# Two partition sums moved behind column tiles, in a one-core hybrid decoder layer

## The chip, the core and the metric

The kernel runs on one core of a Trainium2 chip. The metric is the device time of one execution in microseconds. A core has five engines with a queue each: TensorE (PE in the profile; PEld is its loading of stationary weights), VectorE (DVE), ScalarE (ACT), GpSimd (POOL) and SyncE (SP, which issues DMAs here). TensorE writes its results to PSUM, eight banks of 128 partitions by 512 float32 numbers each; VectorE and ScalarE read them from there ("evacuate" them), GpSimd can't.

## What the kernel computes

One decoder layer on 512 tokens of width 2048, in float32:

```
xn = rms_norm(h, attn_norm_w);  proj = xn @ w_in
y  = [attention(c_q, c_kv, k_rope), conv_module(conv_in), hgrn2(hq, hf, hi, hg)]
h  = h + concat(y) @ w_out
xn = rms_norm(h, ffn_norm_w)
h  = h + (silu(xn @ w_gate) * (xn @ w_up)) @ w_down
return rms_norm(h, final_norm_w)
```

`rms_norm(x, w)` is `x * rsqrt(mean(x*x) + eps) * w`. The factor is one number per token, so it can be put on behind the matrix product: the kernel multiplies the raw `x * w` by the weights and scales each result by the factor, `rstd`, when it evacuates it. The convolution module splits its 1024 columns into `a` and `gate`, forms `a * sigmoid(gate)`, runs a causal convolution of width 31 over the tokens for each of 512 channels, a layer norm over the channels and `silu`. HGRN2 is a gated linear recurrence of four heads.

## The kernel before

Activations lie transposed, channels on the partitions and 512 tokens along the free dimension; a width of 2048 is 16 tiles (`KT`). Each float32 operand is split into a high part (`h`, rounded, by ScalarE, L136 or L139) and a low part (`l`, the rest, by VectorE, L137 or L140), and `mm3` (L143 to L147) forms a product from three matmuls: high by high, high by low, low by high.

`cols_tile` (L149) makes one column tile, 128 output channels by 512 tokens, in one bank of the tag `mm`: 16 k-tiles by 3 are 48 matmuls, with two weight loads of 512 KB. `weights` (L127) loads, splits and hands out these weights; it is traced at a priority 6000 steps ahead of its place, so that loads and splits run ahead as far as the buffers (two raw, three high, three low) allow. `rows_tiles` (L160) makes four banks at once, 192 matmuls.

The order within each engine's queue is fixed when the program is compiled. A planner walks through modelled time and gives each engine the instruction of highest priority that is ready; priority is the place in the program, moved by `high_priority`. The slots of one tag in a pool are handed out in the order of the program. A new area on the same side of memory takes over the place of the closed one, and a tile there waits until the older tiles in its place are done.

The first stage, `first` (L253), loads the 16 tiles of `x` and computes four column tiles of the convolution (`banks[0]` to `banks[3]`: gate and a of the blocks 0 and 1) in the four `mm` banks, k by k, 192 matmuls. Beside it ScalarE squares each `x` tile and GpSimd adds the squares to `acc` (L273). `x_norm` (L279) then sums `acc` over the partitions with a matmul by a matrix of ones (`sum_over_partitions`, L195, bank tag `ax` with two slots), runs `rsqrt` (L180, Ln and Exp on ScalarE, a Newton step on VectorE, then a copy on GpSimd) into `rstd`, and forms the same sums as a column for each token (L286, eight small matmuls, the other `ax` slot) into `rstd_r`. All of it is traced 2000 steps ahead of its place.

`conv_tile` (L435) evacuates a gate bank times `rstd` (L438), forms the sigmoid, evacuates the `a` bank (L443) and runs the 31 taps on VectorE (L449) at a priority 3000 steps behind its place. Blocks 2 and 3 get their banks from two `cols_tile` each. Then come the four banks of the values (tags `lv`, `lv`, `mm`, `mm`; `lv` has two slots), the four of the gate rows, the end of the convolution module with two more sums over the partitions (L452 to L471), and the four HGRN heads, whose tiles (area `hgrn`) take the place of the convolution's (area `conv`). Each head starts with two column tiles (`q`, L337, and `z`, L339).

Later, `project` (L663) makes the 16 column tiles of `w_out`, adds them to `h` and squares the result in the same manner (L680, L681). `project_end` (L684) sums the squares, forms the factor and copies it into `rstd` (L693); its scratch lies in the area `rest`. `token_sums` (L697 to L719), on VectorE and ScalarE, forms sums of quarters of `h` for a product scheme with fewer multiplications; its scratch (area `sum`) takes the place of `rest`. Two plain tiles of the feed-forward stage follow (`ff_plain`, a gate and an up tile each, four column tiles of 48), then 42 fast ones (`ff_fast`), whose first loads (L748) and whose outputs lie where `hf` was, the tile that `token_sums` reads. The lines that the change touches:

Of the kernel before, what the change touches and what calls it, by code (L numbers as in the profile page):

```python
# [92 lines left out]
class Trunk:  # L93
# [52 lines left out]
        mm(out, a[0], b[1], start=False, stop=False, **k)  # L146
        mm(out, a[1], b[0], start=False, stop=last, **k)  # L147

    def cols_tile(self, w, rhs):  # L149

        bank = self.ps("mm")
        n = len(rhs)
        for k0 in range(0, n, 8):
            h, l = self.weights(next(w))
            for k in range(k0, k0 + 8):
                s = slice((k - k0) * P, (k - k0 + 1) * P)
                self.mm3(bank, (h[:, s], l[:, s]), rhs[k], k == 0, k == n - 1)
        return bank
# [117 lines left out]
                self.mm3(banks[j], (h[:, s], l[:, s]), self.x[k], k == 0, k == KT - 1)  # L276
        return banks

    def x_norm(self, r1):  # L279
        nc = self.nc  # L280
        t = [r1(i) for i in ("rv", "ry", "rq")]
        total = self.sum_over_partitions(self.acc)
        nc.gpsimd.tensor_copy(self.rstd, self.rsqrt(total, D, "eps", *t))
        bank = self.ps("ax")
        for c in range(NB):
            nc.tensor.matmul(bank[:, c:c + 1], self.acc[:, c * P:(c + 1) * P], self.ones[:, :1],  # L286
                             start=True, stop=True)
        nc.vector.tensor_copy(self.rstd_r, self.rsqrt_small(bank[:, :NB], D))
# [438 lines left out]
        nc.vector.tensor_tensor(u, u, g, op=ALU.mult)  # L727
        nc.sync.dma_start(self.ffd[f], u)

    def ff_plain(self, f, w, fp):  # L730
        nc = self.nc
        gbank = self.cols_tile(w, self.hw)
        ubank = self.cols_tile(w, self.hw)
        g, u = fp("g"), fp("u")
        nc.vector.tensor_tensor(g, gbank, self.rstd, op=ALU.mult)
        self.last_silu = nc.scalar.activation(g, g, AF.Silu)
        nc.vector.tensor_tensor(u, ubank, g, op=ALU.mult)
        nc.sync.dma_start(self.ffd[f], u)
# [157 lines left out]
    def run(self):  # L896
        tc, io = self.tc, self.io
        area = lambda name, bufs, side="left", space=None: Area(tc, name, bufs, side, space)
        stream = lambda name: iter([io[name][i] for i in range(io[name].shape[0])])
        wr, wc, wa = stream("w_rows"), stream("w_cols"), stream("w_attn")  # L900
        self.mix, self.mix_y = [], []
        self.ps = area("banks1", {"mm": 4, "lv": 2, "ax": 2}, space=PSUM)
        self.yd = self.dp.tile([8, P, S], F32, name="yd")
        self.xp = area("xw", {"xh": KT, "xl": KT})
        self.keep = area("keep", {"h": 4, "l": 4, "krh": 1, "krl": 1, "sin": 1, "cos": 1}, "right")
        r1 = area("conv", {"xraw": 3, "xsq": 2, "acc": 1, "vt": 2, "vsig": 2, "cg": 1, "csg": 2, "hpad": 4,
                           "cacc": 4, "csum": 2, "csq": 2, "cmu": 1, "rv": 1, "ry": 1, "rq": 1,
                           "pos": 1, "ang": 1, "rn": 1, "rr": 1}, "right")
        self.consts()
        banks = self.first(r1, stream("w_first"))  # L910
        self.more_consts()
        self.rope_tables(r1)
        with tc.high_priority(offset=2000):
            self.x_norm(r1)
        self.lower_bounds()
        conv = [self.conv_tile(r1, banks[0], banks[1], 0), self.conv_tile(r1, banks[2], banks[3], 1)]
        for i in (2, 3):
            gbank = self.cols_tile(wc, self.x)
            abank = self.cols_tile(wc, self.x)
            conv.append(self.conv_tile(r1, gbank, abank, i))  # L920
        self.hgrn_values(wr, r1)
        self.hgrn_gates(wr, r1)
        self.conv_end(r1, conv)
        r1.close()
        r2 = area("hgrn", {"lmask": 1, "vh": 2, "gh": 1, "ps": 2, "qk": 2, "e": 2, "ls": 1, "st": 1, "E": 4,
                           "kr": 1, "state": 1, "og": 1, "lt": 5, "la": 1, "lb": 1, "lv_": 1}, "right")
        self.lmask = r2("lmask", I32, (P, len(LEVELS) * 64 + P))
        self.nc.gpsimd.dma_start(self.lmask, io["lmask"])
        for i in range(HG):
            self.hgrn_head(r2, wc, i)  # L930
        cq = self.latent(wc, r2, "lt")
        self.latent_norm(cq, r2)
        self.cq = self.latent_split(cq, "q_w", self.keep)
        ckv = self.latent(wc, r2, "lt")
        self.latent_norm(ckv, r2)
        self.k_rope(wc, r2)
        self.xp.close()
        self.mx = area("mix", {"mx": 2 * KT})
        ckvn = area("ckvn", {"h": 4, "l": 4})
        self.ckv = self.latent_split(ckv, "kv_w", ckvn)  # L940
        r2.close()
        self.ps.close()
        self.ps = area("banks2", {"sc": 2, "mm": 3, "tb": 2, "ob": 1}, space=PSUM)
        r3 = area("attn", {"cmask": 1, "v": 8, "knh": 2, "knl": 2, "qnh": 2, "qnl": 2, "qre": 2, "qro": 2,
                           "qraw": 1, "sw": 1, "rt": 1, "p": 3, "pt": 3, "og": 2, "o2": 1, "yr": 1}, "right")
        self.cmask = r3("cmask", F32, (P, P))
        self.nc.gpsimd.dma_start(self.cmask, io["cmask"])
        self.attention(wa, r3)
        r3.close()
        self.keep.close()  # L950
        ckvn.close()
        stat = area("stat", {"rms": 1, "epsv": 1}, "right")
        self.rms, self.epsv = stat("rms"), stat("epsv")
        self.hp = area("hw", {"hh": KT, "hl": KT}, "right")
        whole = area("whole", {"hf": 1}, "right")
        self.hf = whole("hf", F32, (P, KT, S))
        r4 = area("rest", {"acc": 1, "sq": 2}, "right")
        self.project(stream("w_out"), r4)
        self.ps.close()
        self.ps = area("banks3", {"mm": 8}, space=PSUM)  # L960
        self.project_end(r4)
        r4.close()
        self.mx.close()
        sp = area("sums", {"sh": 4, "sl": 4})
        tp = area("sum", {"s": 1}, "right")
        self.ffd = self.dp.tile([NF, P, S], F32, name="ffd")
        wg = stream("w_gu")
        self.token_sums(sp, tp)
        tp.close()
        whole.close()  # L970
        fp = area("gu", {"g": 2, "u": 2, "pa": 2, "pb": 2, "pc": 2}, "right")
        for f in range(PLAIN):
            self.ff_plain(f, wg, fp)
        rp = area("raw4", {"raw": 5, "t2": 1}, "right")
        for f in range(PLAIN, NF):
            self.ff_fast(f, wg, rp, fp)
        rp.close()
        fp.close()
        self.hp.close()
        sp.close()  # L980
        self.ps.close()
        self.ps = area("banks4", {"mm": 6, "ax": 2}, space=PSUM)
        late = area("late", {"h": 1}, "right")
        self.h = late("h", F32, (P, KT, S))
        fp = area("ff", {"fr": 3, "fh": 2 * CF, "fl": 2 * CF})
        lp = area("last", {"wlh": 10, "wll": 10, "mx": 8}, "right")
        r5 = area("ffn", {"v": 1, "y": 1, "sq": 3, "acc": 1}, "right")
        self.down_all(stream("w_down"), fp, r5, lp)
        for a in (r5, lp, fp, late, stat, self.ps):
            a.close()  # L990
# [115 lines left out]
```

## Time and profile before

| | |
|---|---|
| time, median of 3 executions | 2164.87 us (2163.61 to 2164.97) |
| profiled execution, its own time | 2165.62 us |
| its span in the profile | 2163.8 us, mean granted TensorE clock 0.988 of full |
| TensorE busy | 2111.9 us, 98% |
| VectorE, ScalarE, GpSimd busy | 1391.6 (64%), 893.8 (41%), 171.3 us (8%) |
| HBM read, written | 226.24, 24.12 MB, 116 GB/s over the span |

Times of instructions are counted from the start of the span. A row gives what an engine did, at which line of the kernel, on which tiles; in brackets stands how long the engine had been idle before it, and whose work ended that wait. `x2` behind a float32 sum means two instructions for one matmul of the code.

### The profile page before, as it was taken

The page shows a single profiled execution, that of the slowest core. Times are in us where ns is not written, and L with a number is a line of the kernel's source. Part 1 is how long each engine was busy: PE and PEld are TensorE (multiplying, and loading weights), DVE is VectorE, ACT ScalarE, POOL GpSimd, SP SyncE. Part 2 cuts the span into 40 slices and gives each one's busy share as a digit, 9 for nine tenths or more (in the row PEclk, how much of TensorE's full clock was granted, in tenths as well). Part 3 has the DMA queues.
Part 4 walks back from the last instruction along what each step waited for, and adds up shares of the span by engine and source line. Part 5 has one row for each costly group of instructions (what it writes and reads, how often), then busy time and mean ns, then how long its engine had stood idle before and what let it go on. Part 6 is the DMA issues. An engine that isn't in the chain of part 4 may idle for free.

```text
span 2163.8 us, 31928 instructions
## 1 busy us (share of the span) xinstructions
PE 2111.9 (98%) x13060; PEld 1894.6 (88%) x13060; DVE 1391.6 (64%) x1786; ACT 893.8 (41%) x1357; POOL 171.3 (8%) x150
## 2 busy tenths in 40 slices
PE   7999999999999999999999999999997999999997
PEld 6888888878878779999999999999997788888886
DVE  7897785556543377777787777778776443443347
ACT  6324763456453344444444444444443222221223
POOL 4102474100011100000000000000000000000001
PEclk9999999999999999999999999999999999999998
DMA  5233422222153334334433433433435442342332
GB/s 184 96 118 98 147 74 88 90 82 74 49 193 120 121 122 127 117 103 132 126 106 121 132 112 109 132 122 103 127 122 180 136 135 95 135 135 96 101 108 98
DMA packets 89907, 252.43 MB, mean 117 GB/s; under 512 B 9424, under 2 KB 17872, under 8 KB 89760
## 3 DMA queue, kind: packets, MB, share of 16 engines
q1 hardware_dynamic: 76528, 228.00, 33.0%
q10 hardware_dynamic: 13120, 22.03, 2.9%
q8 instruction: 102, 1.67, 0.3%
q0 software_dynamic: 112, 0.36, 0.1%
q14 instruction: 45, 0.37, 0.1%
HBM read 226.24 MB, written 24.12 MB: 116 GB/s over the span
## 4 chain that ended last, share of the span: by engine, by line
PE 92%; DVE 2%; DMA 2%; ACT 2%; POOL 1%; issue 1%; SPq 0%; DVEq 0%; ACTq 0%; POOLq 0%
PE mm L145 28%; PE mm L147 28%; PE mm L146 28%; PE lv L374 1%; PE ob L611 1%; PE lv L147 1%; PE lv L145 1%; PE lv L146 1%; DVE mx L862 1%; PE sc L586 1%; PE sc L587 1%; DMA xraw<-in_x 0%; DMA fr<-ffd 0%; PE tb L603 0%; ACT wh L136 0%
## 5 line engine op out<-in xcount | busy, mean ns | idle before, releaser
L136 ACT CAST wh<-raw 128x1024 fp32r<-128x1024 f32 (+1 forms) x463 | 478.3, 1035 | 834.5 <-PE mm L146 768.2
L137 DVE TENSOR_TENSOR wl<-raw,wh 128x1024 fp32r<-128x1024 f32 (+1 forms) x463 | 566.6, 1225 | 323.0 <-ACT wh L136 322.6
L146 PE MATMUL mm<-sl,wh 128*128 128x256 f32 x1344 | 378.3, 283 | 0.0
L145 PE MATMUL mm<-sh,wh 128*128 128x256 f32 x1344 | 378.1, 283 | 0.0
L147 PE MATMUL mm<-sh,wl 128*128 128x256 f32 x1344 | 373.5, 283 | 0.0
L145 PE MATMUL mm<-hh,wh 128*128 128x256 f32 (+1 forms) x1072 | 307.9, 287 | 0.0
L147 PE MATMUL mm<-hh,wl 128*128 128x256 f32 (+1 forms) x1072 | 307.5, 287 | 0.0
L146 PE MATMUL mm<-hl,wh 128*128 128x256 f32 (+1 forms) x1072 | 307.1, 286 | 0.0
L145 PE MATMUL mm<-fh,wh 128*128 128x512 f32 (+1 forms) x688 | 263.3, 386 | 12.9 <-ACT fh L136 9.7
L146 PE MATMUL mm<-fl,wh 128*128 128x512 f32 (+1 forms) x688 | 264.5, 385 | 0.2 <-DVE fl L137 0.2
L147 PE MATMUL mm<-fh,wl 128*128 128x512 f32 (+1 forms) x688 | 264.0, 384 | 0.0
L145 PEld LDWEIGHTS mm<-sh,wh 128*128 128x128 f32 x1344 | 257.3, 191 | 0.2 <-DVE u L790 0.2
L146 PEld LDWEIGHTS mm<-sl,wh 128*128 128x128 f32 x1344 | 257.5, 192 | 0.0
L147 PEld LDWEIGHTS mm<-sh,wl 128*128 128x128 f32 x1344 | 254.7, 192 | 0.0
L809 DVE TENSOR_TENSOR h<-h,mm 128x512 f32<-128x512 f32 x80 | 54.8, 687 | 238.2 <-PE mm L147 238.2
L146 PEld LDWEIGHTS mm<-hl,wh 128*128 128x128 f32 x1072 | 202.1, 189 | 3.3 <-issue 0.5
L147 PEld LDWEIGHTS mm<-hh,wl 128*128 128x128 f32 x1072 | 201.6, 188 | 2.9
L145 PEld LDWEIGHTS mm<-hh,wh 128*128 128x128 f32 x1072 | 201.7, 188 | 2.7 <-issue 0.2
L145 PE MATMUL mm<-xh,wh 128*128 128x512 f32 x400 | 160.6, 402 | 5.7 <-ACT wh L136 5.7
L145 PEld LDWEIGHTS mm<-fh,wh 128*128 128x128 f32 x688 | 130.6, 190 | 39.5 <-ACT fh L136 9.9
L146 PE MATMUL mm<-xl,wh 128*128 128x512 f32 x400 | 159.0, 397 | 1.3 <-DVE xl L140 1.3
L147 PE MATMUL mm<-xh,wl 128*128 128x512 f32 x400 | 156.9, 395 | 0.0
(330 smaller groups left out, 3242.6 us busy)
## 6 DMA issues: line engine op xcount, KB each, us to landing
raw<-in_w_gu SPq DMA_DIRECT2D x176, 512.0 KB, 4.3
raw<-in_w_down SPq DMA_DIRECT2D x88, 512.0 KB, 3.3
raw<-in_w_cols SPq DMA_DIRECT2D x42, 512.0 KB, 3.3
raw<-in_w_out SPq DMA_DIRECT2D x32, 512.0 KB, 3.3
ffd<-u SPq DMA_DIRECT2D x44, 256.0 KB, 3.9
fr<-ffd ACTq DMA_DIRECT2D x44, 256.0 KB, 3.6
raw<-in_w_rows SPq DMA_DIRECT2D x16, 512.0 KB, 3.3
raw<-in_w_attn SPq DMA_DIRECT2D x14, 512.0 KB, 3.4
```

Source lines behind the costliest of these rows:

```text
L136: nc.scalar.copy(h, src)
L137: nc.vector.tensor_tensor(l, src, h.bitcast(F32), op=ALU.subtract)
L145: mm(out, a[0], b[0], start=first, stop=False, **k)
L146: mm(out, a[0], b[1], start=False, stop=False, **k)
L147: mm(out, a[1], b[0], start=False, stop=last, **k)
L374: nc.tensor.matmul(bank[:, c * 64:(c + 1) * 64], e[:, c * P:(c + 1) * P], ap_of(e, c * P + h, [2 * h, 64 // h], [1, h]), start=True, stop= ...
L586: nc.tensor.matmul(bank[:, :n], q[rs, qs], k[1][rs, :n], start=False, stop=False)
L587: nc.tensor.matmul(bank[:, :n], q[:, qs], k[0][:, :n], start=False, stop=True)
L611: nc.tensor.matmul(obank[:, qs], pt[:, js], vt[h // 4, j][:, hs], start=j == 0, stop=j == i)
L809: nc.vector.tensor_tensor(self.h[:, m], self.h[:, m], bank, op=ALU.add)
L862: nc.vector.scalar_tensor_tensor(o[:, i * n:(i + 1) * n], self.h[:, m + i, ts], self.col("final_w", m + i), r, ALU.mult, ALU.mult)
```

## The change

Two sums over the partitions get a later place in the program. In the first stage, the two column tiles of convolution block 2 are traced ahead of the sum of `acc`, into the two `lv` banks instead of `mm`; the sum itself leaves `x_norm` and the priority that goes with it, while the rest of `x_norm` keeps both. Behind the projection, the first gate tile is traced ahead of `project_end` and handed to `ff_plain`.

```
-    def cols_tile(self, w, rhs):
-        bank = self.ps("mm")
+    def cols_tile(self, w, rhs, tag="mm"):
+        bank = self.ps(tag)
...
-    def x_norm(self, r1):
+    def x_norm(self, r1, total):
         t = [r1(i) for i in ("rv", "ry", "rq")]
-        total = self.sum_over_partitions(self.acc)
...
-    def ff_plain(self, f, w, fp):
-        gbank = self.cols_tile(w, self.hw)
+    def ff_plain(self, f, w, fp, gbank=None):
+        if gbank is None:
+            gbank = self.cols_tile(w, self.hw)
...
         self.rope_tables(r1)
+        early = [self.cols_tile(wc, self.x, "lv") for _ in range(2)]
+        total = self.sum_over_partitions(self.acc)
         with tc.high_priority(offset=2000):
-            self.x_norm(r1)
+            self.x_norm(r1, total)
...
         for i in (2, 3):
-            gbank = self.cols_tile(wc, self.x)
-            abank = self.cols_tile(wc, self.x)
+            gbank, abank = early if i == 2 else [self.cols_tile(wc, self.x) for _ in range(2)]
...
         self.ps = area("banks3", {"mm": 8}, space=PSUM)
+        wg = stream("w_gu")
+        gbank = self.cols_tile(wg, self.hw)
         self.project_end(r4)
...
-        wg = stream("w_gu")
         self.token_sums(sp, tp)
...
-            self.ff_plain(f, wg, fp)
+            self.ff_plain(f, wg, fp, gbank if f == 0 else None)
```

## Rows read from the trace of the kernel before

**Rows 1.** The page, part 1: busy time, share of the span, instructions.
```profile
PE 2111.9 (98%) x13060; PEld 1894.6 (88%) x13060; DVE 1391.6 (64%) x1786; ACT 893.8 (41%) x1357; POOL 171.3 (8%) x150
```

**Rows 2.** Waits of TensorE: line, waited for; us in total, times, longest.
```profile
PE ax L197 <- POOL acc L273: 4.5, 1, 4.5
PE mm L197 <- POOL acc L681: 4.0, 1, 4.0
...
PE ax L399 <- POOL E L393: 2.0, 1, 2.0
```

**Rows 3.** Timeline of TensorE, first place: start us, length us, engine, line, operation.
```profile
41.03 0.39 PE L147 MATMUL mm<-xh,wl 128*128 128x512 f32 x1
45.94 2.08 PE L197 MATMUL ax<-acc,ones 128*128 128x512 f32 x2 [4.53 <-POOL acc L273]
47.81 1.71 PE L286 MATMUL ax<-ones,acc 128*128 128x1 f32 x8
49.38 0.77 PE L145 MATMUL mm<-xh,wh 128*128 128x512 f32 x1
...
62.49 0.39 PE L145 MATMUL mm<-xh,wh 128*128 128x512 f32 x1
```

**Rows 4.** Groups of TensorE up to 41.5 us: count, busy us, mean ns, idle.
```profile
L145 PE MATMUL mm<-xh,wh 128*128 128x512 f32 x47 | 19.4, 413 | 5.7 <-ACT wh L136 5.7
```

**Rows 5.** Busy time by engine, first evacuation to last tap (window, length, engines, clock).
```profile
61.40:186.90 125.50, 125.50 (x555) 103.94 (x554) 120.75 (x159) 36.74 (x43) 11.60 (x6) 1.00 0.32 105
```

**Rows 6.** The same view: two stretches behind the sums; PEclk is third from last.
```profile
43.55:53.79 10.24, 7.85 (x20) 5.85 (x21) 7.82 (x12) 4.48 (x9) 2.26 (x2) 0.50 0.31 102
760.35:763.77 3.42, 3.42 (x9) 2.34 (x8) 1.92 (x3) 1.42 (x3) 0.00 (x0) 0.51 0.10 38
```

**Rows 7.** Timeline, second place: TensorE, ScalarE and VectorE.
```profile
755.48 0.39 PE L147 MATMUL mm<-mx,wl 128*128 128x512 f32 x1
755.68 1.04 ACT L136 CAST wh<-raw 128x1024 fp32r<-128x1024 f32 x1 [4.38 <-PE mm L146]
...
759.82 1.52 PE L197 MATMUL mm<-acc,ones 128*128 128x512 f32 x2 [3.95 <-POOL acc L681]
...
760.38 1.39 PE L145 MATMUL mm<-hh,wh 128*128 128x512 f32 x1
...
766.73 1.22 DVE L710 TENSOR_TENSOR s<-hf 128x1024 f32<-128x1024 f32 x1
```

**Rows 8.** Timeline of VectorE and GpSimd, first place.
```profile
44.09 2.35 DVE L137 TENSOR_TENSOR wl<-raw,wh 128x512 fp32r<-128x512 f32 x2
...
54.31 0.61 POOL L283 COPY rstd<-rv 128x512 f32<-128x512 f32 x1 [8.42 <-DVE r L188]
...
61.40 0.69 DVE L438 TENSOR_TENSOR cg<-mm,rstd 128x512 f32<-128x512 f32 x1 [1.39 <-PE mm L147]
```

**Rows 9.** The chain that ended last, at the convolution's first sum.
```profile
193.90 0.86 PE ax L197 x2
```

**Rows 10.** Timeline of GpSimd and VectorE: convolution's last add, heads' first evacuation.
```profile
186.96 1.29 POOL L458 TENSOR_TENSOR csum<-csum,cacc 128x512 f32<-128x512 f32 x1 [7.62 <-DVE cacc L449]
...
237.85 0.68 DVE L337 TENSOR_TENSOR qk<-mm,rstd 128x512 f32<-128x512 f32 x1
```

**Rows 11.** Groups of ScalarE from 190 to 239 us: one of the gate rows' four.
```profile
L204 ACT ACTIVATE vsig<-vsig 128x512 f32<-128x512 f32 x4 | 2.5, 623 | 0.0
```

**Rows 12.** Before the first fast tile: SyncE, VectorE, TensorE; load issues 785 to 806 us.
```profile
789.06 2.92 SPq L748 DMA_DIRECT2D raw<-in_w_gu  x5
...
798.94 1.23 DVE L779 TENSOR_TENSOR t<-raw 128x1024 f32<-128x1024 f32 x1
...
806.36 0.28 PE L145 MATMUL mm<-hh,wh 128*128 128x256 f32 x1
...
807.46 1.23 DVE L137 TENSOR_TENSOR wl<-t,wh 128x1024 fp32r<-128x1024 f32 x1 [0.21 <-ACT wh L136]
...
raw<-in_w_gu SPq DMA_DIRECT2D x5, 512.0 KB, 6.3
```

## The prediction

> **What bounds the kernel now.** I read the page's shares first: TensorE is busy for 98% of the span [rows 1], so a change pays only where it takes TensorE's idle time away or adds to it. The waits of TensorE are next [rows 2]: the two sums that the change moves each stand behind GpSimd, 4.5 us at the first norm and 4.0 us at the second. That is all there is to win directly, 8.5 us of 2164, plus what the clock costs after each gap. Then the timeline around each place.
>
> First place [rows 3, 4]: the last matmul before the gap is issued at 41.03; 141 of the first stage's 192 matmuls are recorded by then (a few records are missing), so it is k = 11's last, and k = 12 to 15, 48 matmuls, follow the sum. They start at 49.38 and the next tile at 62.49. At full speed a matmul takes 0.226 us (125.50 us for 555, [rows 5]), so 48 would take 10.8; this stretch took 21.2. TensorE was granted half clock (1.2 GHz) from 43.55 to 53.79, after it had stood still since 41.4 [rows 6].
>
> Second place [rows 7]: the last projection matmul is issued at 755.48, the sum at 759.82, the gate tile at 760.38, at half clock until 763.77 [rows 6].
>
> **The first place, part by part.** *What is removed.* TensorE no longer waits for the squares before k = 12. But k = 12's third matmul needs the low part of its weights, and VectorE writes that in the pair of splits at 44.09 to 46.44 [rows 8], the first done near 45.3. So k = 12 to 15 restart at 45.3 instead of 49.38: 2 matmuls fit in before, 46 × 0.226 = 10.4, plus the clock. The price of a gap in clock: at the second place a gap of 3.95 us cost 8 matmuls at 0.427 instead of 0.226, 1.6 us; at the first a gap of 4.5 us cost half of the 7.85 busy us in the slow stretch, 3.9 [rows 6]. I take 1.6 here, as the gap is under 4 us: the first stage ends at 57.3, 5.2 us earlier than now.
>
> *What is moved ahead.* The two column tiles of the third convolution block, 96 matmuls, 21.7 us, to 79.0; their weights are the same stream in the same order, and SyncE's queue gets none of their loads earlier, since the two raw slots set when it issues. Then the sum, 0.86 us at full clock [rows 9]: 79.9. The eight column sums of the norm are not moved by the code and need only the squares. Their PSUM slot is the second of its tag, behind the sum's, and I expect them behind it, under the stall below, at no cost. If they keep their place they cost a restart at 45.94 and 1.5 us (47.81 to 49.38, [rows 3]), 2.2 us more.
>
> *What is added: a stall.* All eight PSUM banks are now taken: four by the first stage, two by the early tiles, two by the norm. None of the six with results can be emptied before `rstd`, as VectorE's first evacuation multiplies by it. Behind the sum TensorE has nothing to do until that evacuation is through. Today `rstd` is written 6.9 us after the sum ends (48.02 to 54.92, [rows 3, 8]), and the evacuation at 61.40 waits for TensorE, not for `rstd`: k = 12 to 15 cover the norm. At the second place the same chain takes 5.4 (761.34 to 766.73, [rows 7]). I take 6.0, between two close ends: `rstd` at 85.9, evacuated 0.7 + 0.1 later, next tile at 86.7. Today it starts at 62.49 + 21.7 = 84.2: 2.5 us later. A stall of 6 us costs clock too, between 1.6 and 3.9; I take 2.7, the middle, since the two gaps priced are both shorter. TensorE is 5.2 us late.
>
> *What is late next.* The convolution on VectorE starts at the first evacuation, 85.9 instead of 61.40, 24.5 us later. From there to the last tap VectorE is busy for 120.75 of 125.50 us [rows 5], so it can't catch up: the last tap moves from 186.9 to 211.4, and the add behind it from 188.25 to 212.8 [rows 10]. Today that add is early: its sum on TensorE runs at 193.90, behind the gate rows. Afterwards it is VectorE that decides. From 193.90 it takes 44.6 us until the first evacuation of the HGRN heads, 237.85 + 0.68 = 238.53 [rows 9, 10], whose tiles lie where the convolution's lay. That evacuation frees the bank for TensorE's fifth column tile after the gate rows. TensorE comes to it at 193.90 + two sums of 0.86 + 192 × 0.226 = 239.0: half a microsecond of slack, no more. Part of the 44.6 us is the gate rows' own sigmoid work on ScalarE (four groups of four operations, 2.5 us a group, as [rows 11], and the GpSimd products behind them), which will be mostly done when the late sum comes; I take 8 of these 10 us off. Evacuation at 212.8 + 36.6 = 249.4; TensorE, 5.2 us late, wants it at 244.2: another 5.2 us. Ends: nothing off, 13.2 us; 13.2 us off, none. The clock after this second stall I cost at nothing, because TensorE waits 2.0 us for GpSimd at the first head anyway [rows 2] and the heads set the pace there; if that cover is gone, 1.6. First place together: +10.4 us.
>
> **The second place.** *Removed:* TensorE goes on into the gate tile at 755.71; its operands are the same `hw` tiles, and its first weights were split two tiles ahead. Gone are 755.71 to 760.38 (4.7) and the slow clock (1.6), and the sum (0.86) comes back behind the tile: 5.4 us. The four plain tiles then end at 801.0, not 806.36 [rows 12].
>
> *Late next:* the sum now ends at 755.71 + 10.8 + 0.9 = 767.4 instead of 761.34, 6.1 us later. The token sums on VectorE start the moment the norm is done (766.73, [rows 7]): their scratch lies on the norm's scratch. At their end the loads for the first fast tile are issued (789.06, [rows 12]) because those lie on `hf`. Issue at 795.2, landing 6.3 later at 801.5, cast and split 1.0 + 1.2 and the hand-over [rows 7, 12]: 803.9. So TensorE waits 2.9 us and starts the fast tiles 2.5 us earlier than today, not 5.4. Its third product needs a sum that is ready today at 800.16 [rows 12]; 6.1 later, one split behind and with cast and split it is there at 809.8, TensorE at 803.9 + 48 × 0.118 = 809.6. That leaves 2.3, less 1.6 of clock after the wait: −0.7 us. Ends: −5.4 if none of this binds; +2 if the loads land at twice the median.
>
> **Sum.** 2165.62 us for the profiled execution (span 2163.8, 1.8 around it) +10.4 − 0.7 = 2175.3. That execution is 0.75 over the median of the runs, 2164.87; against the median I predict 2174.6 us.
>
> **Rivals.** *The cover holds.* If the sum runs right behind k = 15, or at the latest before about 40 of the 96 early matmuls (its end by 66), `rstd` is there before TensorE runs out of banks and the convolution is hardly later than today. Then the first place gives −5.2 + 0.9 + 0.9 for the eight column sums, −3.4, and the second between −0.7 and −5.4: about −6.4, 2158.5 us. For it: the planner issues what is ready, and the squares are ready by then. Against it: in program order the early tiles come first, and their weights are ahead of TensorE all along (no gap between 62.49 and the gate rows today). The Trainium skill (Perfetto Trace Analysis, Matmul Optimizations) advises using all eight PSUM banks so that more can run in parallel; by that rule this is the outcome. The rows say that here the eight hold results which nothing may read yet.
>
> *The heads don't wait.* Convolution's end shrinks by 13 us or more: +5.2 − 0.7, 2169.4 us. *It doesn't shrink:* stall of 13.2 us, +18.4 − 0.7, 2182.6 us. *The change doesn't do what it says:* the column sums stay in front of k = 12 and wait for the same squares, so the gap at 41.4 stays: 2.2 us more than forecast, 2176.8 us.
>
> **How the numbers follow.** Forecast 0.42, cover holds 0.16, heads don't wait 0.18, no shrinking 0.12, column sums stay 0.12. A measurement tells about 0.2%, 4.3 us, from no change. Slower: 0.42 + 0.12 + 0.12 and half of the 0.18, less 0.05 because the terms are loose, 0.70; within: the other half, a little of the first rival and of the forecast's lower tail, 0.16; faster 0.14. The range 2161 to 2186 leaves out most of the first rival and a tail above; the forecast's own is 2169 to 2183.
>
> **What would show it.** In the changed kernel's profile: at 41 us a gap of 3 to 4 us that VectorE's split ends instead of GpSimd; the sum of `acc` at about 79; a new idle time of 5 to 7 us on TensorE behind it, ended by VectorE; the last tap near 211; TensorE waiting for VectorE near 245; at the second norm no gap, and 3 us at the first fast tile, ended by ScalarE or VectorE. The prediction is wrong if the sum stands among k = 12 to 15 or early in the early tiles, or if the last tap is still before 195.

## The result, and the profile after

The changed kernel takes 2179.08 us (median of 4 runs, 2177.85 to 2181.16) against 2164.92 (4 runs, 2163.61 to 2165.60): ratio 1.0067, 95% interval 1.005 to 1.0085. That is 14.2 us slower, where 9.7 were forecast (2174.6, range 2161 to 2186). The profiled execution took 2177.85 us, with a span of 2176.1. From `x_norm` to `ff_plain` the numbers of unchanged lines are lower by one (L437 is L438 of before, L336 is L337).

The page's first part, which answers to [rows 1]. TensorE's share fell to 97%:

```profile
PE 2115.4 (97%) x13060; PEld 1896.1 (87%) x13060; DVE 1393.0 (64%) x1786; ACT 895.9 (41%) x1357; POOL 172.1 (8%) x150
```

The waits of TensorE, which answer to [rows 2] (line, waited for; us in total, times, longest):

```profile
PE mm L145 <- ACT csg L207: 5.8, 1, 5.8
PE mm L147 <- DVE wl L137: 4.7, 4, 1.7
PE mm L145 <- DVE cg L437: 4.3, 1, 4.3
PE ax L428 <- DVE og L423: 3.1, 2, 1.6
PE mm L145 <- ACT qraw L527: 2.9, 1, 2.9
PE ax L398 <- POOL E L392: 1.9, 1, 1.9
```

Both waits for GpSimd's `acc` are gone, 8.5 us. In their place stand one of 4.3 us for the first evacuation (L437), one of 5.8 us in front of the heads' fifth column tile, which the profile puts down to the convolution's last sigmoid (`csg`), two inside the heads (L428), and four small ones for split weights, one of which (0.53 us) was there before.

The timeline of TensorE around the first place and at the first head, which answers to [rows 3]:

```profile
43.59 0.50 PE L147 MATMUL mm<-xh,wl 128*128 128x512 f32 x1 [1.64 <-DVE wl L137]
...
75.92 1.02 PE L197 MATMUL ax<-acc,ones 128*128 128x512 f32 x2
76.78 0.95 PE L285 MATMUL ax<-ones,acc 128*128 128x1 f32 x8
81.99 0.76 PE L145 MATMUL mm<-xh,wh 128*128 128x512 f32 x1 [4.27 <-DVE cg L437]
...
210.21 1.02 PE L197 MATMUL ax<-csum,ones 128*128 128x512 f32 x2
...
244.92 0.77 PE L145 MATMUL mm<-xh,wh 128*128 128x512 f32 x1 [5.81 <-ACT csg L207]
```

VectorE on the same stretch, which answers to [rows 8, 10]: the split that TensorE waited for at 43.59, the first evacuation, the last taps, the first evacuation of the heads.

```profile
42.85 2.38 DVE L137 TENSOR_TENSOR wl<-raw,wh 128x512 fp32r<-128x512 f32 x2
...
81.16 0.69 DVE L437 TENSOR_TENSOR cg<-mm,rstd 128x512 f32<-128x512 f32 x1
...
203.26 3.35 DVE L448 SCALAR_TENSOR_TENSOR cacc<-hpad,cols,cacc 128x512 f32<-128x512 f32 x3
...
244.09 0.68 DVE L336 TENSOR_TENSOR qk<-mm,rstd 128x512 f32<-128x512 f32 x1
```

The convolution starts 19.8 us later than before (81.16 against 61.40) and ends 19.8 us later (206.6 against 186.8). The heads' first evacuation, whose tile lies where the convolution's tiles lay, comes 6.2 us later (244.09 against 237.85). It ends at 244.77 and frees the bank for the matmul at 244.92; the sigmoid `csg`, which the matmul doesn't read, happens to end in between, at 244.84.

Where the time went is best read by stages. The view by windows gives the window, its length, the busy time of PE, PEld, DVE, ACT and POOL with counts, the granted clock, the DMA share and GB/s. The windows run from the gap in the first stage to the end of the gate rows; to the fifth tile behind them; to the last transposes of the fourth head; to the first sum of the latents (the stage behind the heads); to the end of the wait for `qraw`; to the last projection matmul; to the third product of the first fast tile; and over the last stage. The fast tiles in between, left out here, take 844.21 us in both. First the kernel before:

```profile
41.41:193.74 152.33, 147.80 (x639) 121.70 (x639) 134.29 (x176) 47.33 (x62) 17.82 (x11) 0.97 0.32 104
193.74:239.00 45.26, 45.26 (x197) 36.80 (x196) 29.11 (x29) 33.38 (x55) 17.59 (x11) 1.00 0.38 123
239.00:370.60 131.60, 129.61 (x746) 112.95 (x745) 92.59 (x146) 75.73 (x155) 80.77 (x80) 0.99 0.30 94
370.60:378.50 7.90, 7.90 (x37) 6.53 (x36) 2.90 (x3) 3.10 (x4) 1.29 (x1) 1.00 0.30 102
378.50:438.25 59.75, 57.37 (x248) 46.11 (x247) 31.83 (x42) 25.22 (x35) 5.59 (x4) 1.00 0.28 90
438.25:755.48 317.23, 313.75 (x1499) 255.79 (x1500) 153.47 (x279) 159.60 (x332) 20.17 (x14) 0.99 0.32 107
755.48:812.01 56.53, 52.58 (x244) 43.22 (x243) 43.67 (x43) 25.08 (x28) 1.38 (x1) 0.97 0.35 117
...
1656.22:2163.80 507.58, 488.81 (x2308) 409.85 (x2308) 230.64 (x316) 135.01 (x180) 6.96 (x8) 0.97 0.37 121
```

The same stages of the changed kernel:

```profile
41.95:192.98 151.03, 145.13 (x634) 119.76 (x634) 123.94 (x166) 46.48 (x60) 11.44 (x8) 0.98 0.32 105
192.98:244.92 51.94, 45.70 (x197) 36.57 (x196) 39.19 (x40) 34.94 (x55) 19.73 (x13) 0.99 0.37 122
244.92:379.20 134.28, 128.92 (x712) 109.70 (x713) 90.73 (x144) 73.84 (x152) 80.17 (x81) 0.95 0.26 79
379.20:394.52 15.32, 15.32 (x70) 12.71 (x69) 3.90 (x4) 4.44 (x5) 1.84 (x2) 1.00 0.37 121
394.52:454.85 60.33, 57.42 (x250) 46.39 (x248) 32.16 (x42) 25.23 (x35) 5.87 (x4) 1.00 0.27 89
454.85:772.05 317.20, 313.71 (x1500) 255.84 (x1500) 154.00 (x279) 159.72 (x332) 20.03 (x14) 0.99 0.32 107
772.05:826.90 54.85, 51.84 (x248) 42.68 (x246) 41.44 (x42) 26.11 (x29) 1.41 (x1) 1.00 0.36 120
...
1671.11:2176.10 504.99, 487.40 (x2308) 409.69 (x2308) 230.04 (x316) 135.07 (x180) 6.96 (x8) 0.98 0.37 121
```

By the ends of the stages: TensorE leaves the gate rows 0.8 us earlier (192.98 against 193.74); loses 6.7 us up to the fifth tile; loses 2.7 us in the heads, although 34 of its matmuls no longer stand beside them (712 against 746); these follow behind the heads and take 7.4 us there (15.32 against 7.90); and loses 0.6 us at the latents. That is 16.6 us at the first place (438.25 to 454.85). The second place gives back 1.7. In the last stage this execution of the changed kernel is 2.6 us shorter: 1.2 us of it are idle time, nearly all in the opening waits for weights (2.92, 0.25 and 0.21 us in the kernel before, 0.79 and 1.47 here), the rest is busy time at a granted clock of 0.98 instead of 0.97. The change doesn't touch that stage, and the medians are 14.2 us apart where these spans are 12.3 apart, so I don't count it to the change.

The second place on TensorE, which answers to [rows 7, 12]. On SyncE the loads of the first fast tile are issued at 812.41, 23.35 us later than before, 6.8 more than the 16.57 by which this stretch starts late:

```profile
773.31 0.47 PE L145 MATMUL mm<-hh,wh 128*128 128x512 f32 x1 [0.87 <-ACT wh L136]
...
784.38 1.02 PE L197 MATMUL mm<-acc,ones 128*128 128x512 f32 x2
...
820.35 0.39 PE L147 MATMUL mm<-hh,wl 128*128 128x256 f32 x1 [1.75 <-DVE wl L137]
...
827.29 0.38 PE L147 MATMUL mm<-sh,wl 128*128 128x256 f32 x1 [0.78 <-DVE wl L137]
```

### The profile page after: what moved, and what is told of

The parts are those of the page before. It is cut to its first block, busy times and chain, and to the rows that moved or that the text cites. A ratio compares the mean times of both kernels' runs of the same rounds, so it can differ in the third digit from the quotient of the medians.

```text
span 2176.1 us, 31917 instructions
## 1 busy us (share of the span) xinstructions
PE 2115.4 (97%) x13060; PEld 1896.1 (87%) x13060; DVE 1393.0 (64%) x1786; ACT 895.9 (41%) x1357; POOL 172.1 (8%) x150
## 4 chain that ended last, share of the span: by engine, by line
PE 87%; DVE 4%; POOL 3%; ACT 2%; DMA 2%; issue 2%; SPq 0%; DVEq 0%; ACTq 0%; POOLq 0%
PE mm L147 27%; PE mm L145 27%; PE mm L146 27%; POOL ps L363 1%; PE lv L145 1%; PE lv L146 1%; PE lv L147 1%; PE ob L610 1%; POOL ps L366 1%; DVE wl L137 1%; DVE mx L862 1%; PE sc L585 0%; PE sc L586 0%; ACT E L362 0%; DMA fr<-ffd 0%
## 5 line engine op out<-in xcount | busy, mean ns | idle before, releaser
L145 PE MATMUL mm<-xh,wh 128*128 128x512 f32 x368 | 148.6, 404 | 16.2 <-ACT wh L136 6.1
L146 PEld LDWEIGHTS mm<-fl,wh 128*128 128x128 f32 x688 | 130.4, 190 | 25.8 <-DVE fl L137 0.4
L147 PEld LDWEIGHTS mm<-fh,wl 128*128 128x128 f32 x688 | 130.3, 189 | 25.3
```

The lines of the kernel that those rows point to most:

```text
L145: mm(out, a[0], b[0], start=first, stop=False, **k)
```

## The experiments

The theory for the first place: the time goes because the convolution on VectorE starts some 20 us later and has only 5.6 us to spare (188.25 to 193.90); the heads, which need its memory, wait, and TensorE with them. The rival: the stall and the half clock at the norm itself cost the time. For the second place: the gap is saved, but the token sums, and the loads behind them, start later by about as much. The rival: the gap was not worth more.

**One place at a time.** The first place alone (the second as before):

```
+        early = [self.cols_tile(wc, self.x, "lv") for _ in range(2)]
+        total = self.sum_over_partitions(self.acc)
         with tc.high_priority(offset=2000):
-            self.x_norm(r1)
+            self.x_norm(r1, total)
```

> Only the first place is changed; the second is as before. Theory (late convolution): the trace of the changed kernel stood 16.6 us behind the old one between the two places (438.25 to 454.85), so this run should take 2164.9 + 16.6 = 2181.5 us, 2179 to 2183. In the trace: the sum of acc at 75.9, the last convolution tap at 206, a wait of about 5.8 us at 245, further waits of 1.4 to 1.9 us in the heads. Rival (the second place costs the time): about 2165 us or less.

Measured: 2183.12 us (2182.56 to 2185.56, 4 runs), ratio 1.0091 (1.0078 to 1.0105) to the kernel before, 2164.92 in that comparison: 18.2 us slower, just above the range expected. The waits of the first place stand in its trace as in that of the change. The second place alone:

```
+        gbank = self.cols_tile(wg, self.hw)
         self.project_end(r4)
...
-            self.ff_plain(f, wg, fp)
+            self.ff_plain(f, wg, fp, gbank if f == 0 else None)
```

> Only the second place is changed. Theory (token sums decide): TensorE saves the gap of 4 us and the slow clock behind it, but the sum ends some 6 us later, the token sums and the loads for the first fast tile with it, and TensorE waits for the first fast tile: 14.9 us behind at the third product in place of 16.6, a gain of 1.7 us, so 2163.2 us, 2162 to 2164. Rival (nothing is late): the whole gap comes out, 5.4 us, 2159.5. Rival (the pair of profiles showed chance only): 2164.9.

Measured: 2162.53 us (2159.51 to 2163.52, 11 runs), ratio 0.9989 (0.998 to 0.9998): 2.4 us faster. So the whole loss is the first place's, and the two add up to 15.8, near the 14.2 of the change.

**The sum in front of the early tiles.**

```
-        early = [self.cols_tile(wc, self.x, "lv") for _ in range(2)]
         total = self.sum_over_partitions(self.acc)
+        early = [self.cols_tile(wc, self.x, "lv") for _ in range(2)]
```

> Only the first place; the two early column tiles keep their lv banks but stand behind the sum of acc, which so runs right behind the first stage's last matmul. Theory (late convolution): sum at about 54.2, rstd at about 59.5, first evacuation near 60.3 (61.4 before), last tap near 186; the 96 early matmuls cover the norm, no stall, the next tile starts at 77.7 in place of 84.2, and the heads don't wait: 6 us off, 2159 us, 2157.5 to 2161. Rival (the early tiles in the lv banks, or the slow clock, cost the heads their time): no better than 2170.

Measured: 2159.15 us (2157.55 to 2162.82, 11 runs), ratio 0.9977 (0.9968 to 0.9986), 5.8 us faster, as expected. The sum runs at 54.45. VectorE's first evacuation of the convolution and of the heads:

```profile
60.05 0.69 DVE L437 TENSOR_TENSOR cg<-mm,rstd 128x512 f32<-128x512 f32 x1
...
229.85 0.68 DVE L336 TENSOR_TENSOR qk<-mm,rstd 128x512 f32<-128x512 f32 x1
```

The convolution starts 1.4 us earlier than before, TensorE has 96 matmuls to do while the norm is formed, and it doesn't wait for the heads' first evacuation. The early tiles and their banks are the same as in the change; what differs is only where the sum stands. This is what the rival "the cover holds" described. The Trainium skill (Perfetto Trace Analysis, Matmul Optimizations) advises using all eight PSUM banks for more parallelism: this run agrees with it, and the change, with the same eight banks in use, does not, since there six hold results that nothing may read before the norm. No run has the early sum without the two extra banks.

**The sum between the two early tiles.**

```
-        early = [self.cols_tile(wc, self.x, "lv") for _ in range(2)]
+        early = [self.cols_tile(wc, self.x, "lv")]
         total = self.sum_over_partitions(self.acc)
+        early.append(self.cols_tile(wc, self.x, "lv"))
```

> Only the first place; the sum of acc stands between the two early column tiles, so the convolution on VectorE starts about 10 us later than with the sum in front of both and about 10 us earlier than with it behind both; the second early tile (10.9 us) covers the norm, so there is no stall of TensorE at the norm. Theory (the late convolution makes the heads wait): first evacuation near 71, last tap near 196.5, a wait of 3 to 5 us at the first head's evacuation, part of it given back by the 6 us that the missing gap is worth: 2166 us, 2161 to 2172, between the 2159 of the sum in front and the 2183 of the sum behind. Rival (the loss comes from the stall and the slow clock at the norm, which are gone here): 2159, as with the sum in front.

Measured: 2170.44 us (2169.47 to 2173.81, 6 runs), ratio 1.0029 (1.0018 to 1.004), the kernel before 2164.25 in that comparison: 6.2 us slower. The first evacuation is at 71.15; TensorE has no stall at the norm; its longest waits between 190 and 455 us:

```profile
PE mm L145 <- ACT csg L207: 7.2, 1, 7.2
PE mm L145 <- ACT qraw L527: 2.6, 1, 2.6
```

The rival falls: with no stall at the norm the kernel still loses. The three places of the sum make a scale: first evacuation at 60.05, 71.15 and 81.98, time 5.8 us faster, 6.2 slower, 18.2 slower. Each step of 11 us at the start costs 12 us, but that is no rule of proportion: the last taps end at 186.0, 200.0 and 207.6, and the second step has the stall at the norm in it. The wait for `csg` is longer here than the forecast 3 to 5, because TensorE, which did not stall, came to it earlier.

**A shorter convolution.** The last 7 of the 31 taps are left out, in the kernel with the first place alone and in the kernel before:

```
-            for j in range(1, CONV_W):
+            for j in range(1, CONV_W - 7):
```

> First place as in the change (second as before), and of the convolution's 31 taps the last 7 are left out in each of the four blocks: 28 VectorE operations of 0.73 us, 20.4 us less, which ends the convolution near 186 as in the kernel before. Stall and slow clock at the norm stay. Theory (late convolution): the wait at 245 and those in the heads go, about 0.8 us better than before, 2164 us, 2162 to 2167. Rival (the stall at the norm and what it does to the clock cost the time): 2175 or more.

> The kernel before with the same 7 taps left out in each block. Theory: the convolution had 5.6 us to spare before its sum on TensorE (188.25 to 193.90), which stands behind the gate rows, so taps are worth nothing there: 2164.9 us, 2163 to 2166. Rival (VectorE's taps pace the kernel before too): 2155 or less.

Measured: 2165.87 us (2161.98 to 2167.55, 10 runs), ratio 1.0002 (0.9993 to 1.0011), and 2165.60 (2162.88 to 2166.77, 10 runs), ratio 1.0003 (0.9994 to 1.0012). Seven taps are worth nothing in the kernel before and 17 us with the first place changed (2183.12 to 2165.87). TensorE's longest waits between 190 and 455 us in the first of the two:

```profile
PE ax L398 <- POOL E L392: 1.9, 1, 1.9
PE mm L145 <- ACT qraw L527: 1.7, 1, 1.7
```

The waits for `csg` and `og` are gone, the stall at the norm (4.27 us) is still there. So the late convolution is the cause, of the waits in the heads too, and the stall at the norm by itself costs about what the removed gap was worth. What exactly holds the heads' first evacuation back is not shown. VectorE has idle times of 4.34, 3.08 and 2.26 us between 207 and 240 us of the changed kernel, so its load does not hold it back; the evacuation runs right behind its last product of the convolution (243.48). That the memory is the reason is read from the program; whether the fixed order in VectorE's queue would do the same without it was not tested.

**The second place: shorter token sums.** Three of the four combinations of each round left out, in the kernel with the second place alone and in the kernel before:

```
-            tt(q(0, 1), q(0, 0), q(0, 1), op=ALU.subtract)
-            tt(s1, s1, q(0, 0), op=ALU.subtract)
...
-            tt(q(1, 0), q(1, 0), s1, op=ALU.subtract)
```

> Only the second place, as in the change (sum behind the whole gate tile), and in each of the two rounds of the token sums three of the four combinations are left out: 6 VectorE operations of 1.22 us, 7.3 us less before the loads of the first fast tile are issued. Theory (token sums decide): the loads are issued near 787.5 in place of 794.85, the wait at the first fast tile and the one at the third product go, and the gain grows from 2.4 us to about 5 us: 2160 us, 2158.5 to 2161.5. Rival (the 2.4 us are all that the gap was worth, the rest lost elsewhere): 2162.5.

> The kernel before with the same combinations left out. Theory: TensorE does not wait for the first fast tile there, so the shorter token sums are worth nothing: 2164.9 us, 2164 to 2166. Rival (they pace that stretch before too): 2162 or less.

Measured: 2158.62 us (2155.13 to 2159.70, 6 runs), ratio 0.9969 (0.9957 to 0.9981), 5.5 us faster than the kernel before (2164.14 there); and 2164.78 (2161.66 to 2167.25, 11 runs), ratio 1.0002 (0.9993 to 1.001). The waits of TensorE from 750 to 830 us with the second place alone, first with the full token sums, then with the shortened ones:

```profile
PE mm L147 <- DVE wl L137: 2.5, 2, 1.7
PE mm L145 <- ACT wh L136: 0.9, 1, 0.9
```

```profile
PE mm L145 <- ACT wh L136: 0.9, 1, 0.9
```

The loads are issued at 788.17 instead of 794.85 and the wait for the first fast tile's weights is gone. The missing 3 us were lost to the later token sums, since the shorter ones gain nothing in the kernel before.

**The norm in the middle of the gate tile.** The same work, with the sum and the norm issued when part of the tile is done (the order that results has 32 of its 48 matmuls in front of the sum):

```
                 self.mm3(bank, (h[:, s], l[:, s]), rhs[k], k == 0, k == n - 1)
+            if then and k0 == 0:
+                then()
...
-        gbank = self.cols_tile(wg, self.hw)
-        self.project_end(r4)
+        gbank = self.cols_tile(wg, self.hw, then=lambda: self.project_end(r4))
```

> Only the second place; the sum and the norm stand in the middle of the first gate tile, behind about two thirds of its 48 matmuls. Theory (token sums decide): the gap is filled, the sum ends near 763.8 in place of 761.3 (old) and 767.4 (sum behind the whole tile), loads for the fast tiles issued near 791.5, ready at about 800, when TensorE comes to them at 801: nearly the whole 5.4 us, 2160 us, 2158.5 to 2161. Rival (gain lost elsewhere than in the token sums): like the sum behind the tile, 2163.

Measured: 2159.60 us (2157.23 to 2162.27, 11 runs), ratio 0.998 (0.9971 to 0.9989), 5.3 us faster. TensorE has no wait at the first fast tile. Counted from the last projection matmul, the loads of that tile are issued after 33.6 us in the kernel before, 40.4 with the sum behind the whole tile, and 37.3 here (756.78 to 794.08): the gap is filled, and the loads come early enough. Against the sum behind the whole tile, run beside it, the mean of 11 runs is 2.3 us lower; single runs overlap.

**Both mended**, the sum in front of the early tiles and the norm in the middle of the gate tile, the two diffs together:

> Both places mended: the first with the sum in front of the two early tiles, the second with the sum and the norm in the middle of the first gate tile. The two gains alone were 5.8 and 5.3 us. If they add: 2153.8 us, 2152 to 2156. Rival (they share a later limit): 2158.

Measured: 2155.20 us (2154.86 to 2157.23, 5 runs), ratio 0.9958 (0.9944 to 0.9971) to 2164.25: 9.1 us faster than the kernel before and, across two comparisons, 23.9 below the changed one. The two gains add to 11.1; the interval (6.3 to 12.1 us) holds that as well as less.

## Why the prediction was right or wrong

*Direction and mechanism: right; the sizes of the terms: in part luck.* The stall behind the sum, the late last tap, the heads' wait and the given-back gain at the second place are all in the trace, in that order, and the experiments tie the loss to the convolution. But two terms were wrong by 6 and by 11 us, and the total came out near because they have opposite signs.

*Restart of k = 12 to 15: forecast 45.3 and an end at 57.3, measured 43.59 and 54.15.* The pair of splits is itself 1.2 us earlier (42.85 against 44.09), its first half was done by 43.59, 0.7 us into the pair where I had put 1.2, and the clock did not fall after the gap. Two windows of the changed kernel, the first to be held against [rows 6], the second behind the stall at the norm:

```profile
43.55:53.79 10.24, 10.20 (x45) 8.46 (x46) 5.80 (x6) 2.77 (x4) 1.13 (x1) 1.00 0.47 143
81.99:86.40 4.41, 4.41 (x11) 3.44 (x12) 1.39 (x2) 3.46 (x6) 1.03 (x1) 0.50 0.00 0
```

I took 1.6 us of clock for a gap of under 4 us; the gap was 1.64 and cost none.

*The stall at the norm: the step was right, its place and size were off.* The sum ran at 75.92, not 79.0, and from its end at 76.78 the first evacuation came in 4.4 us, not 6.0. The column sums stood behind the sum, as I expected. The half clock behind the stall cost 11 matmuls at about twice their time, 2.2 us against 2.7. Together with the earlier restart (3.1 us) TensorE left the gate rows 0.8 us early, where I had it 5.2 us late: up to there I was 6 us too high.

*The late convolution: right.* Forecast 24.5 us later, measured 19.8, the difference being the earlier sum (3.1) and the shorter way from it to the evacuation (1.6); VectorE could not catch up. The heads' evacuation was through 34.6 us after the convolution's sum started on TensorE (210.21 to 244.77), where I had 36.6. TensorE wanted it 5.1 us earlier than I thought (239.1) and got it 4.6 us earlier, so the stall of 5.8 us is near my 5.2; this nearness is luck too, since both ends moved.

*The term that was mis-sized most* is the next one: "The clock after this second stall I cost at nothing, because TensorE waits 2.0 us for GpSimd at the first head anyway and the heads set the pace there; if that cover is gone, 1.6." From the fifth tile to the end of the wait for `qraw` the way grew by 10.7 us (199.25 to 209.93), with some 1030 matmuls in both. The wait for GpSimd did not shrink (1.9 us) and covered nothing; in the kernel before TensorE is busy for 129.61 of the heads' 131.60 us, which leaves little to cover with. The trace shows two parts of the 10.7 us. TensorE's idle time grew by 3.9 us, mostly two waits for `og` and a longer one for `qraw`. And it was granted half clock (1.2 GHz), while busy throughout, behind the second stall and behind each wait for `og`; in the kernel before only once, behind the wait for GpSimd. First the three stretches of the changed kernel, then the one of the kernel before:

```profile
244.92:250.18 5.26, 5.26 (x12) 4.12 (x13) 2.57 (x5) 3.23 (x6) 3.74 (x6) 0.50 0.61 166
301.62:304.92 3.30, 3.30 (x9) 2.53 (x8) 1.43 (x4) 0.70 (x3) 1.53 (x1) 0.50 0.77 182
352.70:356.00 3.30, 3.30 (x9) 2.57 (x9) 2.83 (x4) 2.05 (x4) 2.48 (x4) 0.50 0.51 133
```

```profile
275.74:279.08 3.34, 3.34 (x14) 2.86 (x12) 3.34 (x3) 2.28 (x6) 3.09 (x4) 0.50 0.00 0
```

At half clock half of the time is lost: 5.9 us against 1.7, which is 4.3 us more; 2.6 of the 5.9 stand behind the second stall itself, where I had nothing. The remaining 2.5 us are busy time at full clock that was not taken apart. The 34 matmuls that moved behind the heads are no loss of their own: the work is the same, and the time they left free was for the most part taken up by waits and half clock. The run with fewer taps has neither the waits for `csg` and `og` nor the half clock behind them, so all of it follows from the late start.

*The second place: forecast −0.7, measured −1.7 between the profiles and −2.4 by itself.* The chain of the loads was right: in the run of this place alone, where the last projection matmul comes 1.0 us earlier than before (754.48 against 755.48), they are issued at 794.85 and the wait is over at 802.79, that is 795.85 and 803.8 on the forecast's scale, which had 795.2 and 803.9. Two small terms were wrong and nearly cancel: the gate tile did not start at once, since ScalarE casts its weights only at 755.68 (it stands in [rows 7]), a wait of 0.87; and the clock did not fall after the wait of 1.75 us (1.00 in the stage 772.05 to 826.90), where I had 1.6 us.

So the total of 9.7 was 4.5 us short of 14.2: at the first place 6 us too many up to the end of the gate rows (the restart and the stall at the norm), 1.5 too few up to the fifth tile (6.7 against 5.2) and 10.7 too few behind it; at the second 1 to 1.7 too few saved. The rival "the heads don't wait" fell. "The cover holds" was the right picture of the kernel with the sum moved to the front; I priced its first place at 3.4 us, and it is worth 5.8.

## What to carry to other kernels

Filling a wait of the busiest engine delays whoever needs the awaited result: before moving a sum behind other work, read how much room the engine that starts on it has (here VectorE had 5.6 us and was moved by 20). Put the fill on both sides: let the sum run as soon as its input is there, between pieces of independent work, so that the gap before it and the latency behind it are both covered. Behind a late start, count also the further waits that it causes, and the half clock behind them: here some 8 us, beside the first wait of 5.8.

## What was not expected of the hardware

Whether a short gap costs TensorE's clock was not settled by its length alone. After idle times of 1.64, 1.62, 1.70 and 2.05 us near 44 us, in the changed kernel and in three of the first place's variants, and of 2.44 us with both places mended, it stayed at full clock. In the run with 24 taps a gap of 1.78 us at the same place was followed by full speed for 1.5 us and then by half clock, at a cost of 1.7 us:

```profile
43.35:45.35 2.00, 2.00 (x8) 1.64 (x9) 2.00 (x2) 0.48 (x1) 1.09 (x1) 0.89 0.00 0
45.35:47.35 2.00, 2.00 (x6) 1.54 (x5) 1.51 (x3) 0.00 (x0) 0.00 (x0) 0.50 0.63 184
```

In the heads of the changed kernel the waits of 1.64 and 1.42 us for `og` were followed by half clock, the one of 1.94 us for GpSimd was not; in the kernel before the same wait, 1.99 us long, was. After the wait of 4.27 us at the norm the clock was at half in each of the three runs that have it.
